# Six edits at once in a float32 transformer block: order of weight sums, blocks of w_out, first loads, 1/rms

## The chip, the cores and the metric

The kernel runs on one core of a Trainium2 chip. The metric is the device time of one execution in microseconds (us); smaller is better. The engines are TensorE (PE; PEld is its weight load), VectorE (DVE), ScalarE (ACT), GpSimd (POOL) and SyncE (SP), whose queue issues most of the transfers (DMA). Each engine runs its instructions in the order in which they stand in its program and waits at an instruction until what it needs is there.

## The reference

One block of a transformer on x of 512 tokens by 1024 features, in float32:

```python
x = x + 0.5 * swiglu(rmsnorm(x, norm_ffn1), w_ffn1_gate, w_ffn1_up, w_ffn1_down)
x = x + hybrid_mixer(rmsnorm(x, norm_mix), w_in, ..., w_out, rel_bias)
x = x + 0.5 * swiglu(rmsnorm(x, norm_ffn2), w_ffn2_gate, w_ffn2_up, w_ffn2_down)
return rmsnorm(x, norm_final)
```

with `swiglu(h) = (silu(h @ w_gate) * (h @ w_up)) @ w_down`, 2816 hidden features (22 blocks of 128). `hybrid_mixer` projects h by `w_in`, runs block-sparse attention (MoBA) on 8 heads and compressed, selected and windowed attention (NSA) on 8 others, heads of 64, and multiplies the concatenated heads by `w_out` (1024 x 1024).

## The kernel before

**Number format.** Each float32 operand is split into two parts, hi (a rounded copy, by ScalarE, line 91 for weights, 226 for the feed-forward pairs) and lo (the rest, by a VectorE subtraction, lines 95 and 227; by GpSimd, line 93, during the mixer). `mm3` (lines 100 to 102) makes one product of three matmuls: hi by hi, hi by lo, lo by hi. A product over 1024 features is 8 `mm3`, 24 matmuls.

**Layout.** x is kept transposed in eight tiles `x0` to `x7` (128 features by 512 tokens). `gained` makes `xo`, the hi and lo of x times the gain of the norm. The factor 1/rms, R, is one number for each token. It is applied after the products, so they can start before R is known: `rms` sums the squares (`acc`) over partitions by four small matmuls `pr` (line 175), takes root and reciprocal, and spreads the result by four transposes `pR` (line 181) and a copy to R (line 182).

**A feed-forward block** (class `Ffn`, twice: `ffn` with wg1, wu1 and with wg2, wu2). Blocks f = 0 to 3 of the hidden features are plain: gate and up products (`pgu`, 24 matmuls of 512 columns each), then times R (`t`, line 281), silu, product with up (line 283), and split into `h` (line 255). The other 18 blocks go in nine pairs by a scheme with seven products for eight (`pair`): VectorE makes sums S1 to S4 of quarters of the weights (`aw`, line 303) and sums of x (`xa`, `xb`, `xc`, `xd`, `th3`, `tl3`), each quarter or sum is split into `sph` and `spl`, and each of 14 steps is 12 matmuls of 256 columns into `pu`, `pv`, `pw`. VectorE puts the results together (lines 327 to 349; line 339 is one such `t`). The down products `pd` of four earlier blocks are mixed between the steps, and line 487 adds each to x. `go` walks over the steps; it issues the loads 12 steps ahead, the sums 6 ahead and the halves 4 ahead. The tiles `aw` rotate through 16 buffers, two pairs' worth.

**The mixer's end.** `w_out(d, k0, k1)` is one of 32 jobs in a list that fills PE's time beside attention: it loads a piece of 128 KB of w_out, splits it (256 columns wide), makes two `mm3` into one bank `pw` and adds it to x (line 774). A job waits until its heads are done. The last eight jobs take heads 4 to 7. `out_halves` splits the result of a head, `po`, into hi and lo of `kvn` by four steps: ScalarE hi (line 819), VectorE difference `to` (820), ScalarE copy `u` of the second part (822), GpSimd sum to lo (823):

```python
            nc.scalar.activation(hi[b], o[:64], AF.Copy)
            nc.vector.tensor_tensor(t[b], o[:64], f32(hi[b]), ALU.subtract)
            nc.scalar.activation(u[b], o[64:], AF.Copy)
            nc.gpsimd.tensor_tensor(lo[b], t[b], u[b], ALU.add)
```

**What sets the order.** A scheduler orders each engine's instructions from the written program; `tc.issue_after(i)` holds what is written under it behind instruction i. At the start SP issues x0, gcol and then in turn quarters of the first gate and up weights and further x; eight matmuls on a tile of ones (`wake`) run on PE before the first product. The raw weights rotate through four buffers, their halves through five.

Of the kernel before, what the change touches and what calls it, by code (L numbers as in the profile page):

```python
# [29 lines left out]
def block_kernel(ctx: ExitStack, tc: tile.TileContext, A: dict, out: bass.AP):  # L30
# [47 lines left out]
    side = [False]  # L78

    def halves(src):  # L80

        n, width = src.shape[1:]
        per = S // width
        out = []
        for k in range(0, n, per):
            m = min(per, n - k)
            hi, lo = [
                wp.tile([128, S], F32R, name=name, tag=name, bufs=bufs)[:, :m * width].rearrange(
                    "p (a b) -> p a b", a=m) for name, bufs in (("whi", 5), ("wlo", 5))]
            v = src[:, k:k + m]  # L90
            nc.scalar.activation(hi, v, AF.Copy)  # L91
# [20 lines left out]
    first_w = [chunk((8, 128)) for _ in range(2)]  # L112
    for k in range(NK):
# [43 lines left out]
    def squares(tmp, k, tag, bufs):  # L157

        if k == 0:
            nc.scalar.activation(acc, xs[k], AF.Square)  # L160
        else:
            s = tmp.tile([128, S], F32, name="sq", tag=tag, bufs=bufs)
            nc.scalar.activation(s, xs[k], AF.Square)
            nc.vector.tensor_tensor(acc, acc, s, ALU.add)

    summed = [None]
    turned_R = [None]

    def rms(ptag):


        with tc.high_priority():
            p = pt(ptag, "pr")
            for i in range(NT):
                summed[0] = nc.tensor.matmul(p[:, i:i + 1], acc[:, i * 128:(i + 1) * 128], ones_f[:, 0:1],
                                             start=True, stop=True)
            nc.scalar.activation(rc, p[:, :NT], AF.Sqrt, bias=eps, scale=1.0 / D)
            nc.vector.reciprocal(rc, rc)
            p = pt(ptag, "pR")
            for i in range(NT):  # L180
                nc.tensor.transpose(p[:, i * 128:(i + 1) * 128], rc[:, i:i + 1].to_broadcast([128, 128]), ident)
            turned_R[0] = nc.scalar.activation(R, p, AF.Copy)
# [4 lines left out]
    class Ffn:  # L187
# [14 lines left out]
        def __init__(self, wg, wu, which, tmp, hp, sp):  # L202
# [3 lines left out]
            self.behind_rms = None  # L206
# [18 lines left out]
        def halves_of_x(self, hi, lo, v):  # L225
            nc.scalar.activation(hi, v, AF.Copy)  # L226
            nc.vector.tensor_tensor(lo, v, f32(hi), ALU.subtract)  # L227
# [30 lines left out]
        def plain(self, f):  # L258
# [10 lines left out]
            def halves_of(m):  # L269
                got[m] = halves(got[m])  # L270
# [18 lines left out]
        def pair(self, f):  # L289
# [8 lines left out]
            def sums(m, name):  # L298
# [4 lines left out]
                nc.vector.tensor_tensor(to, x, y, op)  # L303
# [65 lines left out]
        def down(self, w, fs, then, tag="mm", groups=(1,) * NK):  # L369
# [9 lines left out]
            def halves_of(d):  # L379
                if d % (4 // n) == 0:  # L380
                    i = d * n % 8
                    for k, v in enumerate(halves(raw[d * n // 8][:, i:i + 4])):
                        got[d + k // n, k % n] = v
# [27 lines left out]
        def lay(self, wd):  # L411
# [3 lines left out]
            self.steps += self.down(wd[0], range(FP), half_added, None, (4, 4))  # L415
# [39 lines left out]
    def bias_rows(hp):  # L455
# [14 lines left out]
        def make():  # L470
            nc.vector.tensor_tensor(tabs[0:32, :], tabs[0:32, :], far, ALU.subtract)
            for oh, h0, c, m in parts:
                p = pt(None, "pb")
                nc.tensor.matmul(p[:16 - h0, :m], tabs[:, h0:16], oh[:, :m], start=True, stop=True)
# [14 lines left out]
    with ExitStack() as ph:  # L489
# [6 lines left out]
        for _ in range(8):  # L496
# [5 lines left out]
        ffn.behind_rms = 1, 1  # L502
# [3 lines left out]
        def after(i):  # L506
            if i == 1:
                with tc.issue_after(made[0].ins):
# [42 lines left out]
    with ExitStack() as ph:  # L551
# [81 lines left out]
        def token_major(key, src, width, tiles):  # L633
# [5 lines left out]
            def chunk_of(k0):  # L639
                k1 = min(k0 + per, NK)  # L640

                def body(w):
# [11 lines left out]
                    for i in range(NT):  # L654
# [4 lines left out]
                        if wide < width:  # L659
                            with tc.issue_after(turned_R[0].ins):  # L660
# [105 lines left out]
        def w_out(d, k0, k1):  # L766
            def body(w):
                while any(2 * k + 1 not in out_done for k in range(k0, k1)):
                    yield
                p = pt("mm", "pw")  # L770
                for k in range(k0, k1):
                    mm3(p, w[k - k0], oT[k], k == k0, k == k1 - 1)
                    yield
                nc.vector.tensor_tensor(xs[d], p, xs[d], ALU.add)
                if k1 == 4:
                    got["x", d] = gained(d, 2)
                    squares(tmp, d, "t", 6)
            return A["w_o"][d][:, k0:k1], body
# [27 lines left out]
        def out_halves(h):  # L806
# [16 lines left out]
            nc.gpsimd.tensor_tensor(lo[b], t[b], u[b], ALU.add)  # L823
# [146 lines left out]
        for i in range(4):  # L970
            fill += [proj(2 * i, moba_t("q", i)), proj(2 * i + 1, moba_t("k", i))]
            if i == 2:
                fill += [w_out(d, 4, 6) for d in range(NK)]
        fill += [w_out(d, k, k + 2) for k in (6, 0) for d in range(NK)]
        last = [w_out(d, 2, 4) for d in range(NK)]
# [63 lines left out]
    with ExitStack() as ph:  # L1039
# [5 lines left out]
        ffn.behind_rms = 1, 0  # L1045
# [96 lines left out]
def _laid_out(x, norm_ffn1, w_ffn1_gate, w_ffn1_up, w_ffn1_down, norm_mix, w_in, cmp_pos_k, cmp_w1_k,  # L1142
# [22 lines left out]
        "w_o": _blocks(w_out[0], D, 128),  # L1165
# [29 lines left out]
```

## Time and profile before

| | |
|---|---|
| median of 3 runs | 1009.53 us (1008.88 to 1009.92) |
| profiled execution, its own time | 1011.25 us |
| its span, first to last instruction | 1009.5 us |
| mean granted TensorE clock | 0.996 |
| PE busy | 983.8 us (97%) |
| VectorE busy | 776.9 us (77%) |
| ScalarE busy | 564.9 us (56%) |
| GpSimd busy | 137.3 us (14%) |

The profile is of one execution. Busy is the time in which an engine has an instruction running. Matmuls overlap, and the ends of matmuls are modelled, so a start says more than a duration.

### The profile page before, as it was taken

The page shows a single profiled execution, that of the slowest core. Times are in us where ns is not written, and L with a number is a line of the kernel's source. Part 1 is how long each engine was busy: PE and PEld are TensorE (multiplying, and loading weights), DVE is VectorE, ACT ScalarE, POOL GpSimd, SP SyncE. Part 2 cuts the span into 40 slices and gives each one's busy share as a digit, 9 for nine tenths or more (in the row PEclk, how much of TensorE's full clock was granted, in tenths as well). Part 3 has the DMA queues.
Part 4 walks back from the last instruction along what each step waited for, and adds up shares of the span by engine and source line. Part 5 has one row for each costly group of instructions (what it writes and reads, how often), then busy time and mean ns, then how long its engine had stood idle before and what let it go on. Part 6 is the DMA issues. An engine that isn't in the chain of part 4 may idle for free.

```text
span 1009.5 us, 17013 instructions
## 1 busy us (share of the span) xinstructions
PE 983.8 (97%) x6080; PEld 871.0 (86%) x6080; DVE 776.9 (77%) x1578; ACT 564.9 (56%) x1181; POOL 137.3 (14%) x193
## 2 busy tenths in 40 slices
PE   8999999999999999999999999999999999999996
PEld 6779999999999898787878888788899999999995
DVE  6797888788766488758888978779878888776744
ACT  6463654454444266557677977655455445444436
POOL 0000000000000000036555776300000000000002
PEclk9999999999999999999999999999999999999998
DMA  7254544233501125541011322425244232341102
GB/s 244 87 197 153 186 149 113 98 101 89 161 25 54 45 85 177 165 127 38 20 45 32 93 65 84 140 86 209 69 144 142 86 105 91 120 146 43 33 11 84
DMA packets 53513, 104.53 MB, mean 104 GB/s; under 512 B 10513, under 2 KB 19170, under 8 KB 53428
## 3 DMA queue, kind: packets, MB, share of 16 engines
q1 hardware_dynamic: 53428, 103.44, 32.6%
q8 instruction: 48, 0.79, 0.3%
q14 instruction: 37, 0.30, 0.1%
HBM read 97.98 MB, written 5.30 MB: 102 GB/s over the span
## 4 chain that ended last, share of the span: by engine, by line
PE 82%; DVE 11%; DMA 3%; issue 2%; ACT 1%; POOL 0%; SPq 0%; DVEq 0%; ACTq 0%; POOLq 0%
PE pd L102 6%; PE pd L100 6%; PE pd L101 6%; PE pu L100 6%; PE pu L102 5%; PE pu L101 5%; PE pw L100 4%; PE pw L101 4%; PE pw L102 4%; PE pp L102 3%; PE pgu L100 3%; PE pp L100 3%; PE pp L101 3%; PE pgu L101 3%; PE pv L100 3%; PE pgu L102 3%
## 5 line engine op out<-in xcount | busy, mean ns | idle before, releaser
L226 ACT ACTIVATE sph<-aw 128x512 fp32r<-128x512 f32 x252 | 155.7, 628 | 138.0 <-PE pu L101 68.1
L91 ACT ACTIVATE whi<-raw 128x512 fp32r<-128x512 f32 (+2 forms) x216 | 124.6, 589 | 151.3 <-PE pd L101 71.8
L227 DVE TENSOR_TENSOR spl<-aw,sph 128x512 fp32r<-128x512 f32 x252 | 170.0, 685 | 49.5 <-ACT sph L226 47.9
L101 PE MATMUL pd<-h,whi 128*128 128x512 f32 x336 | 131.9, 392 | 1.4 <-DVE h L255 1.4
L102 PE MATMUL pd<-h,wlo 128*128 128x512 f32 x336 | 130.9, 390 | 0.8 <-DVE wlo L95 0.6
L95 DVE TENSOR_TENSOR wlo<-raw,whi 128x512 fp32r<-128x512 f32 (+1 forms) x168 | 110.9, 671 | 23.9 <-ACT whi L91 22.6
L100 PE MATMUL pd<-h,whi 128*128 128x512 f32 x336 | 129.0, 392 | 0.0
L100 PE MATMUL pu<-th,sph 128*128 128x256 f32 x432 | 121.5, 281 | 1.1 <-DVE t L339 1.1
L303 DVE TENSOR_TENSOR aw<-aw 128x512 f32<-128x512 f32 x144 | 97.6, 683 | 31.7 <-DMA aw<-in_wg 13.6
L102 PE MATMUL pu<-th,spl 128*128 128x256 f32 x432 | 121.1, 280 | 0.0
L101 PE MATMUL pu<-tl,sph 128*128 128x256 f32 x432 | 121.0, 280 | 0.0
L487 DVE SCALAR_TENSOR_TENSOR x<-pd,x 128x512 f32<-128x512 f32 x88 | 59.9, 685 | 44.7 <-PE pd L102 44.4
L100 PEld LDWEIGHTS pu<-th,sph 128*128 128x128 f32 x432 | 81.6, 189 | 2.8 <-DVE t L339 1.3
L101 PEld LDWEIGHTS pu<-tl,sph 128*128 128x128 f32 x432 | 81.9, 190 | 1.1
L100 PE MATMUL pw<-xo,sph 128*128 128x256 f32 x288 | 80.8, 281 | 0.8 <-DVE x L487 0.5
L102 PEld LDWEIGHTS pu<-th,spl 128*128 128x128 f32 x432 | 81.2, 188 | 0.1
L101 PE MATMUL pw<-xo,sph 128*128 128x256 f32 x288 | 80.4, 280 | 0.0
L102 PE MATMUL pw<-xo,spl 128*128 128x256 f32 x288 | 79.7, 280 | 0.0
L102 PEld LDWEIGHTS pd<-h,wlo 128*128 128x128 f32 x336 | 63.1, 188 | 14.1 <-DVE wlo L95 1.2
L101 PEld LDWEIGHTS pd<-h,whi 128*128 128x128 f32 x336 | 63.3, 188 | 12.8 <-DVE h L255 2.2
L100 PEld LDWEIGHTS pd<-h,whi 128*128 128x128 f32 x336 | 62.9, 188 | 11.1
L100 PEld LDWEIGHTS pw<-xo,sph 128*128 128x128 f32 x288 | 54.1, 188 | 2.6 <-ACT sph L226 1.6
(245 smaller groups left out, 2454.5 us busy)
## 6 DMA issues: line engine op xcount, KB each, us to landing
aw<-in_wg SPq DMA_DIRECT2D x72, 256.0 KB, 3.8
aw<-in_wu SPq DMA_DIRECT2D x72, 256.0 KB, 3.6
raw<-in_wd1a SPq DMA_DIRECT2D x20, 512.0 KB, 4.7
raw<-in_wd2a SPq DMA_DIRECT2D x20, 512.0 KB, 4.8
raw<-in_w_a SPq DMA_DIRECT2D x16, 512.0 KB, 4.4
raw<-in_w SPq DMA_DIRECT2D x8, 512.0 KB, 3.7
raw<-in_w_o SPq DMA_DIRECT2D x32, 128.0 KB, 2.2
raw<-in_wg SPq DMA_DIRECT2D x7, 512.0 KB, 3.8
```

Source lines behind the costliest of these rows:

```text
L91: nc.scalar.activation(hi, v, AF.Copy)
L95: nc.vector.tensor_tensor(lo, v, f32(hi), ALU.subtract)
L100: nc.tensor.matmul(p, w[0], v[0], start=first, stop=False, skip_group_check=again)
L101: nc.tensor.matmul(p, w[0], v[1], start=False, stop=False, skip_group_check=again)
L102: nc.tensor.matmul(p, w[1], v[0], start=False, stop=last, skip_group_check=again)
L226: nc.scalar.activation(hi, v, AF.Copy)
L227: nc.vector.tensor_tensor(lo, v, f32(hi), ALU.subtract)
L303: nc.vector.tensor_tensor(to, x, y, op)
L487: nc.vector.scalar_tensor_tensor(xs[d], p, 0.5, xs[d], ALU.mult, ALU.add)
```

## The change

1. The sums of weights (`sums`) and the splitting of the down weights that are mixed among the pairs stand behind the last `lo` written before them (`behind_lo`).
2. w_out is laid out on the host in blocks of 512 KB (four tiles of x by two of k). 32 jobs become 8, `w_out(g, k0, last)`; halves are 512 wide. In the last two jobs the four products of the first k come before those of the second, into banks of two kinds.
3. The lo sum of head 7, the last head, is made by VectorE.
4. ScalarE's queue issues the two halves of the first gate weights; SP issues all of x and then the first up weights. The up weights are split behind the last `xo`, the squares behind that split.
5. 12 wake matmuls for 8.
6. In both feed-forward blocks the `pr` matmuls stand before the fifth `mm3` of f=1's gate product, the `pR` transposes before f=1's up product. (Before: the sums ahead of f=1's up product in the first block, of its gate product in the second, and no place given for the transposes.) The small matmuls `pb` for the bias rows stand behind `pr`.

```diff
@@ first loads
+    for h in four:
+        nc.scalar.dma_start(first_w[0][:, h], A["wg1"][0][:, h])
     for k in range(NK):
...
         if k == 0:
             nc.sync.dma_start(gcol, A["gcol"])
-        if k < 4:
-            i, h = k % 2, slice(4 * (k // 2), 4 * (k // 2) + 4)
-            nc.sync.dma_start(first_w[i][:, h], A[("wg1", "wu1")[i]][0][:, h])
+    for h in four:
+        nc.sync.dma_start(first_w[1][:, h], A["wu1"][0][:, h])
@@ class Ffn
+            self.last_lo = nc.vector.tensor_tensor(lo, v, f32(hi), ALU.subtract)
+        def behind_lo(self):
+            return tc.issue_after(self.last_lo.ins) if self.last_lo else nullcontext()
...
             def run(m):
                 p = got["p", m] = pt(None, "pgu")
-                with tc.issue_after(summed[0].ins) if (f, m) == self.behind_rms else nullcontext():
-                    for k in range(NK):
+                for k in range(NK):
+                    gate = self.rms_at.get((f, m, k))
+                    with tc.issue_after(gate[0].ins) if gate else nullcontext():
                         mm3(p, got[m][k], self.xg[k], k == 0, k == NK - 1)
...
-                nc.vector.tensor_tensor(to, x, y, op)
+                with self.behind_lo():
+                    nc.vector.tensor_tensor(to, x, y, op)
...
-        for _ in range(8):
+        for _ in range(12):
...
-        ffn.behind_rms = 1, 1
+        ffn.x_made = made[0]
+        ffn.rms_at = {(1, 0, 4): summed, (1, 1, 0): turned_R}
...
-            if i == 1:
-                with tc.issue_after(made[0].ins):
+            if i == 0:
+                with tc.issue_after(ffn.first_up.ins):
@@ output projection
-        def w_out(d, k0, k1):
+        def w_out(g, k0, last=False):
             def body(w):
...
+                for i, k in [(i, k) for k in range(2) for i in range(4)] if last else [
+                        (i, k) for i in range(4) for k in range(2)]:
+                    if k == 0:
+                        ps[i] = pt("mm" if not last or i < 2 else "s", "pw")
+                    mm3(ps[i], w[2 * i + k], oT[k0 + k], k == 0, k == 1)
...
-            nc.gpsimd.tensor_tensor(lo[b], t[b], u[b], ALU.add)
+            (nc.vector if h == 7 else nc.gpsimd).tensor_tensor(lo[b], t[b], u[b], ALU.add)
...
-        ffn.behind_rms = 1, 0
+        ffn.rms_at = {(1, 0, 4): summed, (1, 1, 0): turned_R}
```

What the scheduler makes of it on the engines is shown at three places. On PE, ahead of the second plain block of the first feed-forward block, `pr` moved 12 matmuls and `pR` 20 matmuls up.

The first place is VectorE around the split of the last plain block's `h` in the first feed-forward block (`h_641` before, `h_645` after). Before:

```order
L283 TENSOR_TENSOR t_635<-t_635,t_634 128x512
L303 TENSOR_TENSOR aw_870<-aw_870,aw_918 128x512
L217 TENSOR_TENSOR xc_588<-xa_587 128x256
L227 TENSOR_TENSOR xo_675<-xa_587,xo_674 128x256
L303 TENSOR_TENSOR aw_894<-aw_894,aw_942 128x512
L227 TENSOR_TENSOR xo_677<-xb_589,xo_676 128x512
L255 TENSOR_TENSOR h_641<-t_635,h_640 128x512
```

Of the change:

```order
L234 TENSOR_TENSOR spl_761<-aw_444,sph_760 128x512
L234 TENSOR_TENSOR spl_821<-aw_501,sph_820 128x512
L319 TENSOR_TENSOR aw_446<-aw_446,aw_550 128x512
L234 TENSOR_TENSOR spl_826<-aw_548,sph_825 128x512
L319 TENSOR_TENSOR aw_503<-aw_503,aw_607 128x512
L234 TENSOR_TENSOR xo_679<-xc_592,xo_678 128x256
L234 TENSOR_TENSOR spl_831<-aw_605,sph_830 128x512
L266 TENSOR_TENSOR h_645<-t_639,h_644 128x512
```

The sums of the second pair (`aw_870`, `aw_894`) are gone from here; those of the first pair, which stood 9 and 13 rows ahead of `h`, now stand three and five rows ahead, and the four `spl`, which followed `h`, precede it.

The second place is VectorE at the end of the first pair (line 339, after the change line 355, adds a finished product). Before:

```order
L330 TENSOR_TENSOR t_914<-pw_925,wc_998 128x256
L303 TENSOR_TENSOR aw_1161<-aw_1161,aw_1210 128x512
L227 TENSOR_TENSOR spl_1038<-aw_868,sph_1037 128x512
L303 TENSOR_TENSOR aw_868<-aw_870,aw_868 128x512
L303 TENSOR_TENSOR aw_1185<-aw_1185,aw_1234 128x512
L339 TENSOR_TENSOR t_1034<-pu_835,wc_962 128x256
```

Of the change:

```order
L346 TENSOR_TENSOR t_918<-pw_929,wc_1002 128x256
L234 TENSOR_TENSOR spl_1042<-aw_872,sph_1041 128x512
L355 TENSOR_TENSOR t_1038<-pu_839,wc_966 128x256
L234 TENSOR_TENSOR spl_1060<-aw_896,sph_1059 128x512
L319 TENSOR_TENSOR aw_874<-aw_874,aw_922 128x512
L355 TENSOR_TENSOR t_1057<-pu_857,wc_984 128x256
```

The three sums that stood ahead of the finished product's `t` are gone from ahead of it; the sum of the third pair (`aw_1161`) now stands some 35 rows later.

The third place is PE behind the last attention product `po`. Its result becomes `kvn_7521` and `kvn_7522` (hi and lo) before, `kvn_7513` and `kvn_7514` after. Before:

```order
L107 MATMUL po_7529<-tl_7514,vm_4844 128x128
L100 MATMUL pw_7764<-kvn_7421,whi_7718 128x512
L101 MATMUL pw_7764<-kvn_7422,whi_7718 128x512
L102 MATMUL pw_7764<-kvn_7421,wlo_7719 128x512
L100 MATMUL pw_7783<-kvn_7421,whi_7732 128x512
L101 MATMUL pw_7783<-kvn_7422,whi_7732 128x512
L102 MATMUL pw_7783<-kvn_7421,wlo_7733 128x512
L100 MATMUL pw_7764<-kvn_7521,whi_7718 128x512
L100 MATMUL pw_7783<-kvn_7521,whi_7732 128x512
L101 MATMUL pw_7764<-kvn_7522,whi_7718 128x512
```

Of the change, from the seventh matmul behind `po` on (the six ahead of it are of other heads):

```order
L101 MATMUL pw_7680<-kvn_7413,whi_7566 128x512
L102 MATMUL pw_7680<-kvn_7414,whi_7566 128x512
L103 MATMUL pw_7680<-kvn_7413,wlo_7567 128x512
L101 MATMUL pw_7680<-kvn_7513,whi_7566 128x512
L101 MATMUL pw_7688<-kvn_7513,whi_7570 128x512
L101 MATMUL pw_7692<-kvn_7513,whi_7570 128x512
L101 MATMUL pw_7684<-kvn_7413,whi_7566 128x512
L102 MATMUL pw_7684<-kvn_7414,whi_7566 128x512
L103 MATMUL pw_7684<-kvn_7413,wlo_7567 128x512
L101 MATMUL pw_7684<-kvn_7513,whi_7566 128x512
L102 MATMUL pw_7680<-kvn_7514,whi_7566 128x512
```

The first use of lo is the ninth matmul behind `po` before, the seventeenth after. On ScalarE a split of the next feed-forward block's first weights stands between the steps `kvn` and `u` of this head after the change; on VectorE its lo part stands between `to` and the sum.

## Rows read from the trace of the kernel before

**Rows 1.** Page, busy us (share of the span) xinstructions of each engine.

```profile
PE 983.8 (97%) x6080; PEld 871.0 (86%) x6080; DVE 776.9 (77%) x1578; ACT 564.9 (56%) x1181; POOL 137.3 (14%) x193
```

**Rows 2.** Windows: stretch, its length, busy us of each engine, PEclk, DMA share, GB/s.

```profile
50.00:75.00 25.00, 23.52 (x103) 18.76 (x102) 25.00 (x50) 14.79 (x31) 0.00 (x0) 1.00 0.56 203
75.00:100.00 25.00, 23.89 (x177) 22.52 (x176) 19.94 (x36) 8.95 (x18) 0.00 (x0) 1.00 0.44 140
625.00:650.00 25.00, 22.60 (x107) 17.92 (x106) 16.88 (x27) 15.81 (x31) 11.58 (x14) 1.00 0.38 121
700.00:725.00 25.00, 23.81 (x130) 20.05 (x129) 23.13 (x43) 8.05 (x16) 0.00 (x0) 1.00 0.05 15
750.00:775.00 25.00, 23.79 (x185) 22.65 (x185) 19.82 (x37) 13.56 (x30) 0.00 (x0) 1.00 0.44 145
800.00:825.00 25.00, 25.00 (x169) 23.03 (x168) 18.48 (x34) 10.77 (x22) 0.00 (x0) 1.00 0.36 113
```

**Rows 3.** PE's waits: what waited, for what: us in total, times, longest.

```profile
PE pw L101 <- POOL kvn L823: 1.6, 1, 1.6
PE pd L101 <- DVE h L255: 1.4, 2, 1.1
PE pu L100 <- DVE t L339: 1.1, 1, 1.1
PE pv L100 <- ACT sph L226: 0.9, 1, 0.9
```

**Rows 4.** Timeline of VectorE: start, us, instruction [idle before <-releaser].

```profile
66.76 0.67 DVE L303 TENSOR_TENSOR aw<-aw 128x512 f32<-128x512 f32 x1
67.96 0.67 DVE L255 TENSOR_TENSOR h<-t,h 128x512 fp32r<-128x512 f32 x1
```

**Rows 5.** Timeline of PE, the same stretch.

```profile
67.07 1.29 PE L100 MATMUL pd<-h,whi 128*128 128x512 f32 x5
68.69 0.50 PE L101 MATMUL pd<-h,whi 128*128 128x512 f32 x1 [0.32 <-DVE h L255]
```

**Rows 6.** Timeline of VectorE, first use of R.

```profile
32.23 1.29 DVE L281 TENSOR_TENSOR t<-pgu,R 128x512 f32<-128x512 f32 x2 [1.98 <-ACT R L182]
```

**Rows 7.** Timeline of VectorE, end of the first pair.

```profile
96.14 0.69 DVE L303 TENSOR_TENSOR aw<-aw 128x512 f32<-128x512 f32 x1 [1.88 <-DMA aw<-in_wg]
98.68 0.42 DVE L339 TENSOR_TENSOR t<-pu,wc 128x256 f32<-128x256 f32 x1
```

**Rows 8.** Timeline, all engines, behind the last attention product.

```profile
636.31 0.59 ACT L819 ACTIVATE kvn<-po 64x512 fp32r<-64x512 f32 x1 [0.17 <-PE po L107]
637.01 0.68 DVE L820 TENSOR_TENSOR to<-po,kvn 64x512 f32<-64x512 f32 x1 [0.41 <-POOL wlo L93]
637.73 0.59 ACT L822 ACTIVATE u<-po 64x512 f32<-64x512 f32 x1 [0.82 <-DVE to L820]
638.46 1.26 POOL L823 TENSOR_TENSOR kvn<-to,u 64x512 fp32r<-64x512 f32 x1 [1.49 <-ACT u L822]
639.77 0.50 PE L101 MATMUL pw<-kvn,whi 128*128 128x512 f32 x1 [1.60 <-POOL kvn L823]
```

**Rows 9.** Timeline of PE, SP and ScalarE, start of the kernel.

```profile
1.47 3.78 PE L497 MATMUL wake<-ones 128*128 128x512 f32 x8 [1.47 <-DVE ones L136]
...
1.65 0.43 SPq L121 DMA_DIRECT2D raw<-in_wg  x1
...
6.39 0.79 PE L100 MATMUL pgu<-xo,whi 128*128 128x512 f32 x1 [1.15 <-ACT whi L91]
...
12.87 1.38 ACT L147 ACTIVATE xo<-x,gcol 128x512 fp32r<-128x512 f32 x2 [0.19 <-DMA x<-in_xT]
...
19.81 0.39 PE L100 MATMUL pgu<-xo,whi 128*128 128x512 f32 x1
```

**Rows 10.** Chain that ended last, start of the kernel: start, us, what.

```profile
7.61 0.43 PE pgu L102
```

More of the change, by code (lines that the diff above doesn't have):

```diff
@@ L78, in block_kernel @@
     side = [False]
+    last_hi = [None]
     def halves(src):
@@ L163, in squares @@
             nc.scalar.activation(s, xs[k], AF.Square)
-            nc.vector.tensor_tensor(acc, acc, s, ALU.add)
+            added[0] = nc.vector.tensor_tensor(acc, acc, s, ALU.add)
+    added = [None]
     summed = [None]
-    turned_R = [None]
+    turned_R, copied_R = [None], [None]
     def rms(ptag):
@@ L367, in pair, with down @@
             return steps
-        def down(self, w, fs, then, tag="mm", groups=(1,) * NK):
+        def down(self, w, fs, then, tag="mm", groups=(1,) * NK, kept_back=True):
             n = len(fs)
@@ L381, in halves_of @@
                     i = d * n % 8
-                    for k, v in enumerate(halves(raw[d * n // 8][:, i:i + 4])):
+                    with self.behind_lo() if kept_back else nullcontext():
+                        parts = halves(raw[d * n // 8][:, i:i + 4])
+                    for k, v in enumerate(parts):
                         got[d + k // n, k % n] = v
@@ L414, in lay @@
                 self.steps += self.plain(f)
-            self.steps += self.down(wd[0], range(FP), half_added, None, (4, 4))
+            self.steps += self.down(wd[0], range(FP), half_added, None, (4, 4), False)
             fills = []
@@ L470, in make @@
         def make():
-            nc.vector.tensor_tensor(tabs[0:32, :], tabs[0:32, :], far, ALU.subtract)
+            with tc.issue_after(added[0].ins):
+                nc.vector.tensor_tensor(tabs[0:32, :], tabs[0:32, :], far, ALU.subtract)
             for oh, h0, c, m in parts:
                 p = pt(None, "pb")
-                nc.tensor.matmul(p[:16 - h0, :m], tabs[:, h0:16], oh[:, :m], start=True, stop=True)
+                with tc.issue_after(summed[0].ins):
+                    nc.tensor.matmul(p[:16 - h0, :m], tabs[:, h0:16], oh[:, :m], start=True, stop=True)
                 if h0:
@@ L764, in block_kernel @@
         out_done = set()
-        def w_out(d, k0, k1):
+        def w_out(g, k0, last=False):
             def body(w):
-                while any(2 * k + 1 not in out_done for k in range(k0, k1)):
+                while any(2 * k + 1 not in out_done for k in (k0, k0 + 1)):
                     yield
-                p = pt("mm", "pw")
-                for k in range(k0, k1):
-                    mm3(p, w[k - k0], oT[k], k == k0, k == k1 - 1)
-                    yield
[L774 to L778, printed above, removed]
+                ps = {}
+                for i, k in [(i, k) for k in range(2) for i in range(4)] if last else [
[3 more added lines that the diff above has]
+                    mm3(ps[i], w[2 * i + k], oT[k0 + k], k == 0, k == 1)
+                    yield
+                    if k == 1:
+                        d = 4 * g + i
+                        nc.vector.tensor_tensor(xs[d], ps[i], xs[d], ALU.add)
+                        if last:
+                            got["x", d] = gained(d, 2)
+                            squares(tmp, d, "t", 6)
+            return A["w_o"][k0 // 2, g], body
         def stream(jobs, ahead=3):
@@ L972, in block_kernel @@
             if i == 2:
-                fill += [w_out(d, 4, 6) for d in range(NK)]
-        fill += [w_out(d, k, k + 2) for k in (6, 0) for d in range(NK)]
-        last = [w_out(d, 2, 4) for d in range(NK)]
+                fill += [w_out(g, 4) for g in range(2)]
+        fill += [w_out(g, k) for k in (6, 0) for g in range(2)]
+        last = [w_out(g, 2, True) for g in range(2)]
         work = stream(pre + fill + last)
```

22 lines of the change are left out of this document (14 added, 8 removed).

## The prediction

> **What bounds the kernel now.** I read the page first. TensorE (PE) is busy 983.8 of 1009.5 us and VectorE 776.9, ScalarE 564.9 [rows 1], so the time is the sum of the stretches in which PE stands still, and nearly nothing else can be won. The second view is the table of windows. In a steady stretch of the second feed-forward block, 800 to 825, PE is busy the whole 25.00 us; in 50 to 75, 75 to 100, 625 to 650, 700 to 725 and 750 to 775 it lacks 1.48, 1.11, 2.40, 1.19 and 1.21 us [rows 2]. The reader should see in the same rows that VectorE is busy 25.00 of 25 in 50 to 75: there it sets the pace, and PE waits for whatever stands late in VectorE's queue. The third view, the list of PE's waits, gives the names: the lo half of an attention output added on GpSimd (1.6), `h` of the feed-forward blocks (1.4 in two waits), the `t` of line 339 (1.1), `sph` (0.9) [rows 3]. The fourth, the timeline, says why those are late.
>
> **What the change does to each, and its price.** The span is 1009.5 and the run's own time 1011.25, so 1.75 lie outside; this execution is 1.72 above the median of 1009.53. I make the sum against 1011.25 and take 1.72 off at the end.
>
> *The first feed-forward block.* VectorE works in the order of its program. At 66.76 it makes a sum of weights (0.67) for a pair of blocks that is far from due, and only at 67.96 the `h` that the down products need; PE has run five first products ahead from 67.07 and then idles 0.32 [rows 4, 5]. The order's first excerpt shows four such sums within the dozen or so VectorE rows ahead of `h`, at 0.60 each from one start to the next (66.76 to 67.96 is two): 2.4 us, of which two (those of the second pair) now stand some 40 rows later and the other two follow the first `spl` halves. Also, R (1/rms), which starts VectorE's saturated stretch with the first `t` at 32.23 [rows 6], comes earlier: its transposes stand 20 matmuls further up, 20 x 0.225 = 4.5 us. (0.225 is the pitch of 512-column matmuls in a dense stretch: five are shown as 1.29 [rows 5] and one as 0.39 [rows 9], so 0.90 / 4.) VectorE was late by 1 to 3 rows of 0.6; both shifts are larger. So I expect the 1.48 of this window to go.
>
> In the pairs, a sum at 96.14 made VectorE idle 1.88 for the transfer of its operand, though `t` for PE (98.68) stood behind it [rows 7]; PE then waited 1.1 [rows 3]. The second excerpt's `aw_1161` is that sum, ahead of line 339's `t`; it now stands behind the `spl` of the pair's end. What was hidden by it? Nothing: VectorE has 5 us free in that window (19.94 of 25) [rows 2]. So the 1.11 goes too. Together 2.59, taken at nine tenths: **-2.3** (bounds -1.0, if only the waits behind a transfer go, and -2.6).
>
> *The second block* has the same two places: 1.19 and 1.21 [rows 2]. R gains nothing relative to PE here, since its transposes already stood ahead of the up products; only the sums move. **-2.2** of 2.40 (bounds -0.6 and -2.4).
>
> *The end of the output projection.* After the last attention product the chain is ScalarE 636.31, VectorE 637.01, ScalarE 637.73, GpSimd 638.46 to 639.72, and PE takes it at 639.77: 3.5 us, which eight matmuls (1.8) were meant to cover, and PE waits 1.60 [rows 8]. Now the add is on VectorE. For a 64x512 add there I take 0.68, the duration of VectorE's own 64x512 step in the same chain, against GpSimd's 1.26 [rows 8]: -0.58 on the path. And by the third excerpt sixteen matmuls stand in the gap instead of eight: 3.6 us. Against this, two instructions that the diff doesn't show have slid in: ScalarE's `whi` of the next block's first weights stands between the chain's two ScalarE steps, waiting for PE's last use of a buffer, five matmuls (1.1) behind the last `po`, and then about 0.6, like ScalarE's other 512-wide steps there; VectorE's `wlo` of it (0.6) stands ahead of the add. The chain is then about 1.2 + 0.6 + 0.6 + 0.1 + 0.68 = 3.2, or about 3.3 with `u` beside it, against 3.6: covered, by 0.3. If the cover fails, the 512-wide blocks give nothing here. Of the 2.40 of this window I take **-1.9** (bounds 0 and -2.4); the rest are waits for `x` of line 774, whose 0.68 adds remain.
>
> *The blocks of w_out* themselves: 32 transfers become 8, the same bytes; ScalarE and GpSimd make half as many halves of twice the width. GpSimd's 512-wide step I price at the 1.26 of the 64x512 one. It lies beside PE; cost 0 unless it holds up a scaled softmax row behind it, at most 1.26 a time.
>
> *The start.* Real products begin at 6.39; the first matmul of block f=1 at 19.81; 48 matmuls lie between them, 10.8 us at 0.225, so 2.6 us are lost to waiting and to the slow pitch of 0.43 that the chain shows at first [rows 10], about twice 0.225, as at the lower of TensorE's two levels (1.2 GHz). The gate's weights were issued third, at 1.65, and the last x was awaited at 12.87 [rows 9]. Now ScalarE's queue issues the gate's weights at the very start and up's 512 KB go behind all x. Gate's 24 products then follow x as it lands, and up's 24 (5.4) start when its weights have landed and been halved. The bytes are the same, so the last still land about 12.9 less the two issues of 0.43 saved; 12.0 to 12.9 plus about 0.6 for one half plus 5.4 is 18.0 to 18.9, and a little more, as the last matmuls of the gate may still run. Twelve wake matmuls instead of eight add 4 x 0.43 = 1.7 to the 3.78 us of waking [rows 9, 10] and close the idle 1.15 ahead of the first product; they cost nothing while ScalarE's first `whi` and `xo` are what PE awaits. The two new issues on ScalarE lie in time that it spent waiting for gcol. f=1 at 18.9: **-0.9** (bounds 0, PE stopping once between gate and up, and -1.6).
> The Trainium skill speaks against part of this: "DMA: Bandwidth & Descriptors" (Issuing engines are not separate DMA queues) says that transfers from several issuing engines share the same 16 DMA engines and that only issue time is saved. By that rule alone, with up's weights landing no sooner than the last x did, the start gains about 0.4 and the time would be 1001.8. No row of before has two issuing engines, so the trace doesn't decide it.
>
> *Earlier summed squares.* The four `pr` stand twelve matmuls (2.7 us) further up, and with f=1 0.9 earlier they could meet an unfinished sum of squares: cost 0 to 0.5, inside the start's bounds.
>
> *Restarts.* Each wait costs PE more than the idle shown: five matmuls from 67.07 at 0.225 would let the next start at 68.20; it starts at 68.69, 0.49 later, where 0.32 is shown [rows 5]. Some eight waits go, at about 0.15, three quarters of it: **-0.9** (0 to -1.2).
>
> Sum: -0.9 -2.3 -2.2 -1.9 -0.9 = -8.2. 1011.25 - 8.2 = 1003.05 for an execution like the profiled one; less 1.72: **1001.3**. All upper bounds together: -10.2, 999.3. All lower: -1.6, 1007.9.
>
> **Rivals.** *Half of it* (0.15): VectorE's lateness in the two dense stretches only moves. For it: VectorE is full in 50 to 75, and no edit removes work from it. Against: R comes earlier, and two sums leave the stretch. The feed-forward terms halve, -2.3, and half of the restarts go: about 1004.
> *The projection's cover fails* (0.12): the slid-in `whi` waits longer than five matmuls, for its weights' transfer, and holds `u` behind it. For it: in before the same weights were issued only at about the time of the last `po`; against: a buffer of the 8 large jobs comes free a whole job (24 matmuls, 5.4 us) earlier. Then the 1.9 stays: 1003.2.
> *The start gains nothing* (0.13): the bytes bound it: 1002.2.
> *Slower* (0.07): a sum held behind the last `spl` comes too late for ScalarE's `sph`, and as ScalarE too works in order, every half behind it is late. There are 18 pairs in the two blocks; it decides once a pair loses 0.46 us (8.2 / 18). With 0.7 a pair, 12.6 in all, the time is 1001.3 + 12.6 = 1013.9. Against: sums are asked for six steps ahead and halves four, two steps of 12 matmuls of 256 columns, at half of 0.225, 2.7 us, and VectorE has 20% to spare outside the dense stretch.
> *No effect* (0.03): the sums' place in the queue is not what makes PE wait: 1009.5 within 0.2%, which is 2 us and about what a measurement of this kernel can tell from no change.
>
> **How the numbers follow.** The forecast, 999 to 1003, has 0.50; the three partial rivals 0.40 end between 1002 and 1004.5, or with two of them together near 1006. The range 998.3 to 1006.5 goes from the full bounds, with 1 us for the spread of the runs shown, to two partial failures at once. Faster by over 0.2% (below 1007.5): 0.88; within: 0.05 (no effect, and what is left when the partial ones come together); slower: 0.07.
>
> **What would show it.** Windows 50 to 75 and 75 to 100 (and their like in the second block) with PE near 25.0; no wait of `pd` for `h`, of `pu` for line 339's successor, of `pw` for the lo add. No VectorE idle on an `aw` transfer with `t` behind it. First matmul of f=1 at about 18.9. I'm wrong if a new entry over 1 us heads PE's waits, above all `sph` or `aw` at every pair, or ScalarE's `whi` after the last `po`.

## The result, and the profile after

| | median us | runs | ratio to the kernel before, 95% interval |
|---|---|---|---|
| before | 1009.35 | 1008.88 to 1009.92 (4) | |
| changed | 998.98 | 997.14 to 999.69 (4) | 0.990 (0.9888 to 0.9911) |

The change takes 10.4 us off, 1.0%. The forecast was 1001.3 (8.2 less), range 998.3 to 1006.5. The measured median lies just below the stretch of 999 to 1003 that had the chance of 0.50, and below 999.3, all upper bounds of the sum together; the range holds it because it adds 1 us for the spread of the runs. The profiled execution took 999.69 us, its span is 997.9.

The page's line of busy times (us, share of the span, instructions; [rows 1]):

```profile
PE 979.2 (98%) x6084; PEld 870.7 (87%) x6084; DVE 780.9 (78%) x1579; ACT 566.3 (57%) x1165; POOL 132.6 (13%) x176
```

PE is busy 4.6 us less than before in a span that is 11.6 shorter. The table of windows, with the stretches of [rows 2]:

```profile
50.00:75.00 25.00, 25.00 (x121) 21.03 (x120) 25.00 (x48) 15.01 (x31) 0.00 (x0) 1.00 0.48 171
75.00:100.00 25.00, 25.00 (x195) 24.15 (x194) 17.29 (x31) 11.85 (x24) 0.00 (x0) 1.00 0.54 175
625.00:650.00 25.00, 25.00 (x115) 20.57 (x114) 20.74 (x35) 16.52 (x29) 2.58 (x2) 1.00 0.20 64
700.00:725.00 25.00, 25.00 (x182) 23.58 (x181) 19.34 (x34) 9.81 (x20) 0.00 (x0) 1.00 0.36 108
750.00:775.00 25.00, 24.00 (x176) 22.65 (x177) 23.49 (x43) 15.12 (x30) 0.00 (x0) 1.00 0.41 127
800.00:825.00 25.00, 25.00 (x177) 23.36 (x176) 20.36 (x36) 13.07 (x26) 0.00 (x0) 1.00 0.20 64
```

Four of the five stretches that lacked 1.1 to 2.4 us of PE are full. One wait of about an us is left in 750 to 775. PE's longest waits, to be held against [rows 3]:

```profile
PE wake L517 <- DVE ones L139: 1.5, 1, 1.5
PE ps_t L916 <- DVE th L977: 1.3, 2, 1.0
PE ps_t L916 <- DVE tl L920: 1.2, 1, 1.2
PE pu L101 <- ACT t L361: 1.1, 1, 1.1
PE ps_s L892 <- DVE m L898: 1.1, 6, 0.2
```

None of the four of [rows 3] is there. `ps_t` for `tl`, 1.2, is new and lies in attention; `pu` for ScalarE's `t`, 1.1, is new too, at 751.00. VectorE no longer stands idle ahead of the sums of weights. The page's lines, before and changed (us busy, mean ns of one, then us of idle before them and what ended most of it):

```profile
L303 DVE TENSOR_TENSOR aw<-aw 128x512 f32<-128x512 f32 x144 | 97.6, 683 | 31.7 <-DMA aw<-in_wg 13.6
L319 DVE TENSOR_TENSOR aw<-aw 128x512 f32<-128x512 f32 x144 | 98.2, 683 | 0.0
```

At the start (ScalarE's and SP's queues and PE; [rows 9]):

```profile
0.74 0.90 ACTq L116 DMA_DIRECT2D raw<-in_wg  x2
...
1.47 4.53 PE L517 MATMUL wake<-ones 128*128 128x512 f32 x12 [1.47 <-DVE ones L139]
...
6.11 0.99 SPq L124 DMA_DIRECT2D raw<-in_wu  x2
...
18.41 0.39 PE L101 MATMUL pgu<-xo,whi 128*128 128x512 f32 x1
```

Block f=1 begins at 18.41, 1.40 earlier.

A better view than idle times is where the same matmul of PE stands in time. The table gives, from the timeline of PE, five stretches between such landmarks: **S**, from 0 to the first `pgu` matmul of f=1; **A**, from the first `pd` to the first `pp` (the rest of the first feed-forward block); **M**, from there to the last `po` (mixer); **P**, from there to the 25th `pgu` matmul of the second block (end of the output projection); **F**, from that block's first `pd` to the last.

| | S | A | M | P | F |
|---|---|---|---|---|---|
| before | 19.81 | 303.37 | 275.76 | 19.82 | 305.63 |
| changed | 18.41 | 297.75 | 276.47 | 16.69 | 302.99 |
| difference | -1.40 | -5.62 | +0.71 | -3.13 | -2.64 |
| the prediction's terms | -0.9 | -2.3 | 0 | -1.9 | -2.2 |

The prediction's remaining -0.9 was for restarts in A, P and F.

### The profile page after: what moved, and what is told of

Same layout as the page of the kernel before. It is cut to its first block, busy times and chain, and to the rows that moved or that the text cites. A ratio compares the mean times of both kernels' runs of the same rounds, so it can differ in the third digit from the quotient of the medians.

```text
span 997.9 us, 16910 instructions
## 1 busy us (share of the span) xinstructions
PE 979.2 (98%) x6084; PEld 870.7 (87%) x6084; DVE 780.9 (78%) x1579; ACT 566.3 (57%) x1165; POOL 132.6 (13%) x176
## 4 chain that ended last, share of the span: by engine, by line
PE 92%; DVE 4%; ACT 1%; DMA 1%; issue 1%; SPq 0%; ACTq 0%; DVEq 0%
PE pd L101 8%; PE pd L102 8%; PE pd L103 8%; PE pu L101 6%; PE pu L103 6%; PE pu L102 6%; PE pw L101 5%; PE pw L102 4%; PE pw L103 4%; PE pp L103 3%; PE pgu L101 3%; PE pgu L102 3%; PE pp L101 3%; PE pgu L103 3%; PE pp L102 3%; PE pv L101 3%
## 5 line engine op out<-in xcount | busy, mean ns | idle before, releaser
L233 ACT ACTIVATE sph<-aw 128x512 fp32r<-128x512 f32 x252 | 157.7, 630 | 158.6 <-PE pu L102 74.6
L92 ACT ACTIVATE whi<-raw 128x512 fp32r<-128x512 f32 (+1 forms) x200 | 122.1, 621 | 174.7 <-PE pd L102 88.4
```

The lines of the kernel that those rows point to most:

```text
L92: last_hi[0] = nc.scalar.activation(hi, v, AF.Copy)
```

## The experiments

All medians stand beside those of the kernel before on the same chip, 1009.58 for e1 to e4, 1009.96 for e5 to e8, 1009.78 for e9 to e12. Two versions whose intervals overlap are not told apart by their medians; for these the landmarks of one profile each are given, as what they are. Of the landmarks P and A repeat well where the same code runs: P is 16.69 to 16.71 in seven profiles and 19.81 to 19.86 in four, A 297.63 to 298.09 in the nine that have edits 1 and 6. S and M vary more (see e9 and the last section).

**e1: the order of the sums undone.**

```diff
-                with self.behind_lo():
-                    nc.vector.tensor_tensor(to, x, y, op)
+                nc.vector.tensor_tensor(to, x, y, op)
...
-                    with self.behind_lo() if kept_back else nullcontext():
-                        parts = halves(raw[d * n // 8][:, i:i + 4])
+                    parts = halves(raw[d * n // 8][:, i:i + 4])
```

> The changed kernel with the sums and the kept-back down halves again wherever the scheduler puts them (edit 1 undone), all else kept. Theory A, the place of the sums in VectorE's queue is what made PE wait: of the 8.2 us that the two feed-forward blocks gained (landmarks of PE: 5.6 in the first, 2.6 in the second), 5 to 8 come back, about 1004 to 1007, and waits of PE for h and for t behind a transfer of aw are in the list again. Theory B, the earlier R relieved VectorE and the sums' place is a side matter: 0 to 3 come back, 999 to 1002, and the pairs behind the first stay dense.

1004.23 us, ratio 0.9944 (0.9923 to 0.9964). A is 301.76 (+4.0 against the changed kernel), F 304.73 (+1.7). From PE's waits:

```profile
PE pd L102 <- DVE h L266: 1.8, 2, 0.9
...
PE pu L101 <- DVE t L363: 0.8, 2, 0.6
...
PE pv L103 <- DVE spl L234: 0.7, 2, 0.4
```

Theory A, at its lower edge. The 4.0 are spread: 1.6 us in the dense stretch up to the first pair's middle, 2.4 in the pairs behind it, in waits for `t` and `spl` that end at 120.74, 123.21 and 152.66 and smaller ones.

**e2: edit 6 undone, the rest kept.**

```diff
-        ffn.rms_at = {(1, 0, 4): summed, (1, 1, 0): turned_R}
+        ffn.rms_at = {(1, 1, 0): summed}      # first block
+        ffn.rms_at = {(1, 0, 0): summed}      # second block
```

(the places of the bias products go back as well)

> The changed kernel with edit 6 undone: sums of squares again ahead of the first block's up product of f=1 and of the second block's gate product, no place for the transposes. Theory A: VectorE's dense stretch of the first block (50 to 87) starts later against PE and about 1 to 2 us come back, all of it ahead of the first pair's second half; the second block is unchanged; 1000 to 1001. Theory B: 2.5 us or more come back, 1001.5 or above. If the sums alone suffice: under 0.5 us.

1005.94 us, ratio 0.9964 (0.9952 to 0.9976): 7.0 above the changed kernel's median, 6.5 by the two ratios. Only theory B's open bound (2.5 us or more) holds, and it named no place; theory A held the second block unchanged. A is 301.12, +3.4, of which 2.3 at `h` and 0.7 at a `wlo` behind it. The other half is in a place that I had not thought of, the second block:

```profile
PE pr L179 <- DVE acc L167: 2.0, 1, 2.0
PE pd L102 <- DVE h L266: 2.0, 1, 2.0
```

The windows around it (columns as in [rows 2]; PEclk is the third number from the end):

```profile
657.00:660.00 3.00, 2.09 (x13) 1.86 (x14) 1.04 (x3) 1.01 (x2) 0.00 (x0) 0.95 0.58 175
660.00:663.00 3.00, 3.00 (x9) 2.35 (x8) 0.00 (x0) 0.00 (x0) 0.00 (x0) 0.50 0.03 5
663.00:675.00 12.00, 12.00 (x56) 9.95 (x55) 9.12 (x16) 6.96 (x11) 0.00 (x0) 0.99 0.26 76
```

With the projection's end 3.1 shorter, PE comes to `pr` before the sum of squares is made: it waits 2.0 us, and then its granted clock is 0.50 for about 3.4 us: 9 matmuls in 3 us, where 13 or 14 fit. P is as short as after the change (16.70), but the stretch behind it up to the first `pd` takes 43.3 instead of 39.5. So in this block the edit does not move R ahead, as the first block's does; it moves `pr` twelve matmuls **back**, out of the way of a wait that the faster projection would have made.

**e5 and e6: each of the two alone, on the kernel before.**

> The kernel before with edit 1 alone. With e1 and e2 read: behind the first dense stretch the sums' place alone should bring what e1 lost there, 2.5 to 3 us in the first block's pairs and 1 to 2 in the second block; in the dense stretch of 56 to 77 nothing or a loss, as in e2, where PE waited 2.1 for h. Theory A (place and earlier R help different stretches and only together free the dense one): 1005.5 to 1007.5. Theory B (the place of the sums suffices): 1003 or below.

> The kernel before with edit 6 alone. Theory A: the dense stretch of the first block gains 1 to 2 us, the pairs nothing; in the second block the dense stretch (707 to 714) keeps its wait for h, since R stood ahead of it before too: 1007.5 to 1009. Theory B: the earlier R also moves the pairs' waits: 1005 or below.

e5: 1003.47, ratio 0.9938 (0.9922 to 0.9953), A 299.72 (-3.7 against before), F 301.76 (-3.9). e6: 1008.82, ratio 0.9989 (0.9977 to 1.0002), A 302.96 (-0.4), F 305.14 (-0.5). Their waits, e5 first:

```profile
PE pw L102 <- POOL kvn L841: 1.6, 1, 1.6
...
PE pd L102 <- DVE h L265: 1.0, 1, 1.0
```

```profile
PE pu L101 <- DVE t L353: 2.9, 3, 1.3
...
PE pd L102 <- DVE h L265: 1.6, 2, 0.9
```

The order alone already gives 6.5 us, near theory B's 1003 and below the range of theory A, because the pairs gained more than the 2.5 to 3 expected. The first block shows it in two parts. From the first `pd` to the 197th matmul behind it (in the middle of the first pair, where each kernel has made the same products) the order alone gains 0.3 us on before, the earlier R alone 0.9, both (changed kernel) 2.2. From there to the first `pp` it is 3.3, -0.5 and 3.4. So the gain in the pairs is the order's, and in the dense stretch theory A holds: with the order alone PE still waits 1.0 for `h` there; with the earlier R alone it waits 0.6 (the rest of the 1.6 is in the second block), and 2.9 for `t` in the pairs of both blocks. Only with both (changed kernel, e10) is there no wait for `h`. VectorE's idle time ahead of the sums is 31.6 us in e1 and 27.4 in e6, and 0.0 in e5 as in every other run with the order. e6's gain is not shown by its median.

**e10: the two together, nothing else** (before, with edits 1 and 6).

> The kernel before with edits 1 and 6 together and nothing else. Alone they gave 6.5 and 1.1 in the medians, 7.6. Theory A, they free different stretches and the dense one only together: 7.5 to 9 below before, 1001 to 1002.5. Theory B, with the old start R's gain is not used, since PE too is late: 6.5 or less, 1003.5 or above.

999.88 us, ratio 0.9910 (0.9893 to 0.9927). Above both expectations in its gain: 9.9 us, of 10.4 for all six; e5 and e6 sum to 7.6. By the medians alone this excess is not clear of the intervals; in A the two give 3.7 and 0.4 alone and 5.7 together, in F 3.9 and 0.5 alone and 3.6 together, so it lies in the first block's dense stretch. A is 297.63, the changed kernel's value. P is 19.86, as before. So two edits carry the change; that the other four add something is not shown by the medians (their intervals overlap), though the profile has P 3.2 longer here. Its M is 3.0 shorter than the changed kernel's: 1.6 for a dip of the clock (last section), 1.4 that the blocks cost in attention (e8).

**e3, e4, e9: the start.** e3 undoes edit 4 (the diff's load lines, and the squares behind `made[0]` again), e4 edit 5 (`range(8)`), e9 both.

> The changed kernel with edit 4 undone: gate and up weights again issued by SP between the x, products in turns, squares as before; 12 wake matmuls are kept. My theory: the order of the bytes ahead of x and up gave most of the 1.4 us by which block f=1 starts earlier: 0.8 to 1.4 come back, 999.8 to 1000.4. Rival: the longer waking gave it, by an earlier rise of the pitch, and this run loses under 0.5.

> The changed kernel with 8 wake matmuls. My theory: PE idles about 0.9 between waking and the first product, its pitch stays at 0.43 until about 10 us, but the loads bound the start, so block f=1 starts 0 to 0.6 later: 999.0 to 999.6. Rival: the lower pitch now bounds the gate's products, f=1 starts 1 us or more later: 1000 or above.

> The changed kernel with edits 4 and 5 both undone (8 wake matmuls, weights and x in turns on SP). Undone one by one they cost 0.64 and 0.99 at the start of block f=1 and nothing measurable in the median. Theory A: each alone keeps PE at the short pitch from about 5 us on, both away leave it at 0.43 until 10 us or later, as in before, e5 and e6; f=1 then starts 1.4 to 3 us later (19.8 to 21.5), R comes later too, and 1.5 to 3 us come back: 1000.5 to 1002. Theory B: they simply add, 1.6 at f=1, under 1 us in the median.

Medians 999.13 (ratio 0.9901, 0.9879 to 0.9922), 998.49 (0.9889, 0.9866 to 0.9912) and 999.25 (0.9905, 0.9887 to 0.9924): none can be told from the changed kernel, so the 0.8 to 1.4 expected of e3 did not come. In the profiles f=1 begins at 19.40, 19.05 and 21.52, against 18.41. e9's windows, then the changed kernel's:

```profile
4.00:8.00 4.00, 2.39 (x8) 1.07 (x7) 2.20 (x3) 1.82 (x3) 0.00 (x0) 0.97 0.85 296
8.00:12.00 4.00, 4.00 (x8) 2.48 (x9) 2.93 (x5) 3.68 (x7) 0.00 (x0) 0.50 1.02 381
12.00:16.00 4.00, 4.00 (x13) 3.16 (x13) 3.81 (x7) 3.96 (x8) 0.00 (x0) 0.68 0.91 316
```

```profile
4.00:8.00 4.00, 3.46 (x11) 1.92 (x10) 2.55 (x4) 3.21 (x6) 0.00 (x0) 1.00 1.05 359
8.00:12.00 4.00, 3.86 (x17) 3.08 (x18) 4.00 (x7) 3.63 (x6) 0.00 (x0) 1.00 1.01 340
12.00:16.00 4.00, 4.00 (x19) 3.15 (x18) 2.95 (x6) 3.70 (x8) 0.00 (x0) 1.00 0.79 261
```

With both undone PE's granted clock is 0.50 in 8 to 12, and 8 matmuls start in it instead of 17. e3 and e4 have 12 and 14 there, at a granted clock of 1.00. In the five profiles with the old start (before, e5, e6, e9, e10) f=1 begins at 19.81, 21.21, 21.50, 21.52 and 19.63; in the six with both edits and edit 6 (changed, e1, e7, e8, e11, e12) between 18.41 and 19.00. Either edit is enough for the clock (theory A's mechanism, in one profile each), yet its price in the median, 1.5 to 3, did not come. In e9's profile the later start is not lost on the way: its first `pd` is 2.9 us later than the changed kernel's, its first `pp` 3.2, its last `pd` 2.3. But this is the slowest of e9's six executions (1002.25, mean granted clock 0.990; the others 997.35 to 1001.14 at 0.995 to 0.997), so the profile overstates what the old start costs, and f=1 begins anywhere from 19.63 to 21.52 with it. What it costs in the median is open.

**e7, e11: the end of the projection.** e7 undoes edit 2 (32 jobs of 128 KB), e11 edit 3:

```diff
-            (nc.vector if h == 7 else nc.gpsimd).tensor_tensor(lo[b], t[b], u[b], ALU.add)
+            nc.gpsimd.tensor_tensor(lo[b], t[b], u[b], ALU.add)
```

> The changed kernel with w_out in 32 jobs of 128 KB again (edit 2 undone); head 7's lo sum stays on VectorE. My theory: the wait behind the last attention product comes back less the 0.6 that VectorE's add saves (1.0 to 1.2 of the 1.6), with a wait or two for x: of the 3.1 us won between the last po and the second block's products 1.5 to 2.5 come back; ahead of it, in attention, 0.5 to 1 is won back, as GpSimd's 512-wide steps no longer hold VectorE. 1000 to 1001. Rival, the blocks themselves do nothing for the time and the add did it all: 998 to 999.

> The changed kernel with head 7's lo sum on GpSimd (edit 3 undone). Between the last po and PE's first use of lo stand sixteen matmuls, 3.6 us; the chain of the changed kernel measured against them has to be lengthened by 0.58. If the prediction's chain of 3.2 to 3.3 is right, PE waits 0.2 to 0.4 and the projection's end comes 0.2 to 0.5 later. Rival: the blocks cover it all, no wait. In the median 999 to 999.5, or not to be told from the changed kernel.

e7: 998.23 (ratio 0.9892, 0.9875 to 0.9909), e11: 998.21 (0.9890, 0.9874 to 0.9907); neither median can be told from the changed kernel. P is 19.24 and 17.13, against 16.69 with both edits and 19.82 with neither. So the add alone takes 0.58, the difference between 1.26 and 0.68 of the prediction; the blocks alone 2.69; both 3.13. In the median e7's 1000 to 1001 did not come, and the rival's 998 to 999 did, but not for its reason: the blocks do win at the end. Their waits:

```profile
PE pw L102 <- DVE kvn L845: 1.0, 1, 1.0
...
PE pw L101 <- DVE x L795: 0.8, 2, 0.5
```

```profile
PE pw L102 <- POOL kvn L851: 0.3, 1, 0.3
```

The chain in the changed kernel (all engines, [rows 8]):

```profile
630.15 0.59 ACT L846 ACTIVATE kvn<-po 64x512 fp32r<-64x512 f32 x1 [1.67 <-PE po L108]
...
630.84 0.69 DVE L847 TENSOR_TENSOR to<-po,kvn 64x512 f32<-64x512 f32 x1 [0.41 <-ACT kvn L846]
...
631.40 0.64 ACT L92 ACTIVATE whi<-raw 128x512 fp32r<-128x512 f32 x1 [0.66 <-PE pw L102]
...
632.06 0.59 ACT L849 ACTIVATE u<-po 64x512 f32<-64x512 f32 x1
...
632.19 0.68 DVE L96 TENSOR_TENSOR wlo<-raw,whi 128x512 fp32r<-128x512 f32 x1
...
632.91 0.69 DVE L851 TENSOR_TENSOR kvn<-to,u 64x512 fp32r<-64x512 f32 x1
...
633.43 0.39 PE L101 MATMUL pw<-kvn,whi 128*128 128x512 f32 x1
...
633.74 0.47 PE L102 MATMUL pw<-kvn,whi 128*128 128x512 f32 x1
```

The `whi` and `wlo` that slid in are there, at 631.40 and 632.19, each ahead of a step of the chain. PE's first use of lo starts 0.31 behind the matmul ahead of it, 0.08 more than the pitch: the cover of 3.6 us is used up to the last tenth, where I counted on 0.3 to spare.

And yet e7 is not slower. Its M is 275.14 against 276.47. The blocks give back in attention a part of what they win at the end, and e8 says how. Without the clock's dip (last section) M is 274.89 with the blocks (e4) and 273.49 to 273.65 with small jobs (e5, e6, e10): the blocks cost 1.2 to 1.4 there.

**e8: GpSimd's lo in two halves.**

```diff
-                nc.gpsimd.tensor_tensor(lo, v, f32(hi), ALU.subtract)
+                for c in range(0, m, 2):
+                    nc.gpsimd.tensor_tensor(lo[:, c:c + 2], v[:, c:c + 2], f32(hi[:, c:c + 2]), ALU.subtract)
```

> The changed kernel; GpSimd makes each lo of 512 columns by two instructions of 256. My theory: a VectorE instruction with two operands in SBUF that meets one of GpSimd's waits for its end (aq of line 609 took 1.70 instead of 0.69 beside a GpSimd lo of 1.29); with halves of 0.74 it waits less, 1.2 or below, and PE's wait of 1.2 for tl behind it falls to 0.7 or below; 998.0 to 998.8. Rival, the lengthening has another cause: aq stays at 1.7 and the wait at 1.2.

997.42 us, ratio 0.9879 (0.9862 to 0.9895). The changed kernel's timeline where `ps_t` waits for `tl`, then e8's at the same place:

```profile
594.34 1.29 POOL L94 TENSOR_TENSOR wlo<-raw,whi 128x512 fp32r<-128x512 f32 x1
...
594.48 1.70 DVE L609 TENSOR_TENSOR aq<-t,aq 64x512 fp32r<-64x512 f32 x1
...
596.94 0.69 DVE L609 TENSOR_TENSOR aq<-t,aq 64x512 fp32r<-64x512 f32 x1
...
598.37 0.41 PE L916 MATMUL ps_t<-ident,lpn 128*128 128x128 f32 x2 [1.17 <-DVE tl L920]
```

```profile
592.24 1.88 POOL L95 TENSOR_TENSOR wlo<-raw,whi 128x256 fp32r<-128x256 f32 x2
...
592.38 1.14 DVE L610 TENSOR_TENSOR aq<-t,aq 64x512 fp32r<-64x512 f32 x1
...
595.71 0.41 PE L917 MATMUL ps_t<-ident,lpn 128*128 128x128 f32 x2 [0.60 <-DVE tl L921]
```

In the changed kernel `aq` runs 1.70 beside GpSimd's 1.29 and ends 0.55 behind its end; the next `aq`, 2.5 us later, with no such instruction beside it, takes 0.69. In e8 it takes 1.14, its neighbour being a step of half the width, and PE's wait for `tl` falls from 1.17 to 0.60. The theory's numbers for `aq` and the wait came; the median is below its 998.0 to 998.8, and cannot be told from the changed kernel's. M is 273.81, 1.1 less than in e4, which has no dip of the clock either. That the cause is operands of both engines in SBUF (the memory in which the kernel's tiles lie; products lie in PSUM) fits the other meetings in the changed kernel's trace (last section), but was not tried by itself.

**e12: a version made from the runs.** 128 KB jobs for all but the last eight pieces (`w_small`, the old body on the new layout), blocks for the last two jobs, and e8's halves.

> A version made from the runs: the changed kernel with 128 KB jobs for the first 24 pieces of w_out, as before, and the 512 KB blocks only for the last two jobs; GpSimd's lo of 512 columns in two halves. Theory: attention keeps what e7 and e8 showed (0.6 to 1.3 us), the projection's end keeps its 3.1: 996.8 to 998.0, below both kernels. Rival: the small jobs bring back the wait of 1.1 for t at the end of attention that before and e7 have, and the gain is nil: 998.5 to 999.5.

997.03 us, ratio 0.9878 (0.9862 to 0.9895), the lowest median. It beats the kernel before; its interval touches that of the changed kernel (0.9888 to 0.9911), and e8 is as good. P is 16.18, M 274.62, so it kept P's gain (though PE waits 0.8 for head 7's lo again, at 632.03), but in M, where it was to keep 0.6 to 1.3, it is only 0.3 below e4's 274.89 and behind e8's 273.81; why is open.

## Why the prediction was right, and where its steps were off

*What bounds the kernel.* Right: the gain is PE's waits, which went where the windows had them. Most of it is the order of the sums.

*First feed-forward block, -2.3 and a share of -0.9 for restarts: measured -5.62.* It lies beyond the term's bound of -2.6, even with all of the restarts. The mechanism in the pairs was right, the size was off: I took 1.11 for them, and e5 shows 3.3 by the order alone, from the first pair's middle to the last. I priced it by PE's idle time in two windows. The windows 100 to 125 and 125 to 150 of before show PE busy 24.94 and 25.00 of 25, and yet the same matmuls that take 35.83 us there (102.59 to 138.42) take 34.47 after the change. Eight starts in there come 0.1 to 0.2 late, 1.0 in all, and show as nearly no idle time, since the modelled ends of the matmuls cover them.

In the dense stretch the step "VectorE was late by 1 to 3 rows; both shifts are larger" failed as an argument: the two shifts are not alternatives (0.3 and 0.9 alone, 2.2 together). e5 shows the order alone leaving 1.0 of waiting for `h`, e6 and e1 the earlier R alone leaving 0.6 and 0.9 for it. R comes 4.9 us earlier, but the last `h` only 2.0 (67.96 before, 65.92 after): it follows VectorE's first `t` by 35.7 before and 38.5 after, and by 39.8 in e1 and e6, without the order. With the late R, VectorE's first `t` and that 197th matmul of PE lie 60.6 us apart before (32.23 to 92.81), 59.7 in e2 (33.10 to 92.83) and 60.3 in e5, whenever PE begins; only with edits 1 and 6 together does PE become the bound again: in all nine profiles that have both it takes 33.7 from its first `pd` to that matmul. So a start that is earlier for PE alone is worth nothing there: e2 begins the down products 0.7 earlier than before does and is at 92.83 in the place where before is at 92.81.

*Second block, -2.2: measured -2.64,* and 3.3 to 4.0 in ten other profiles with the sums ordered (F 301.60 to 302.30): the profile of the changed kernel has a wait of 1.1 at 751.00, behind ScalarE's `whi` that waits 3.93 for a transfer of down weights; in e3, e5 and e11 it is not in the list, in e8 and e12 it is 0.4. "The same two places" was a misreading for 750 to 775: of before's 1.21 there, 0.87 is a wait for ScalarE's `sph`, which stands behind a `whi` that waited 1.57 for down weights, and 0.34 one for `spl`. The wait that is left is of the same kind, in ScalarE's queue, although edit 1 also holds that `whi` back behind a `lo`. "R gains nothing relative to PE here" was true for the kernel before, and missed what e2 shows: with the faster projection the old place of `pr` would have cost 3.8 us. This interaction of edits 2 and 6 was in no rival.

*End of the projection, -1.9: measured -3.13.* Right in the mechanism: 0.58 for the add (e7), the rest for the blocks. I took four fifths of the window's 2.40, since I expected waits for `x` to stay; they went too, and the gain is beyond even the bound of -2.4, so here too the idle time was less than the loss. The chain took 3.45 (630.15 to 633.60) for my 3.2 or 3.3. The rival "cover fails" was closer than its 0.12: the margin is nothing.

*The blocks themselves, "cost 0 unless ...".* This term was mis-sized, and by another mechanism than the one named. Not a softmax row behind GpSimd's longer step in its own queue, but VectorE beside it: with the same dip of the clock (below), M is 276.47 against 275.76 and 275.14 with small jobs, 0.7 to 1.3 us; without it 1.2 to 1.4, of which e8 gives 1.1 back.

*Start, -0.9: measured -1.40* in the one pair of profiles, but the medians of e3, e4 and e9 don't show it. That the Trainium skill's "DMA: Bandwidth & Descriptors" (Issuing engines are not separate DMA queues) leaves only issue time to gain is neither borne out nor refuted here: e3, with the old queues and twelve wake matmuls, starts f=1 0.99 later, and no run had the new order of bytes on one queue.

*The rivals.* "Slower", a loss at each of 18 pairs, found nothing: `sph` and `aw` are not in the list of waits. "Half of it" did not come: both feed-forward terms came out larger than taken. "The start gains nothing" is not decided: the medians cannot tell. "No effect" is excluded by the interval.

*The sum.* The blocks' cost and the three terms that came out beyond their bounds do not cancel in the profile (11.6 us for 8.2); that 998.98 still lies in the range is due to the 1 us added for the spread, not to the terms.

## What to carry to other kernels

In an engine that works in order, look for instructions that wait for a transfer and are due much later, and put them behind the last thing somebody waits for; here this alone was 6.5 of 10.4 us. Look at each engine's queue: the wait left at 751.00 is the same thing on ScalarE. Price a wait by where the same instruction of the bound engine stands before and after, not by its idle time: small waits don't show as idle. And when a stretch becomes faster, ask which instruction placed "safely early" behind it now comes too early, as `pr` did.

## What the runs showed of the hardware that was not expected

*The granted clock of PE within a run.* In the profiles of before, changed, e1, e2, e3, e7, e9 and e11 the granted clock falls to half for 3.4 us near 410 us, in e4, e5, e6, e8, e10 and e12 not. Two windows of the kernel before (the second is at 0.51):

```profile
407.00:413.50 6.50, 5.07 (x27) 3.96 (x26) 6.43 (x15) 2.93 (x9) 0.00 (x0) 1.00 0.06 15
413.50:417.00 3.50, 3.50 (x15) 3.11 (x14) 2.61 (x6) 1.26 (x2) 0.00 (x0) 0.51 0.83 241
```

In 407 to 413.5, ahead of it, PE stood still for 1.4 of 6.5 us. That alone does not decide it: in the 6.5 us at the same distance from the first `pp` all fourteen profiles have the same 27 matmuls and 1.42 to 1.44 us of standing still, and eight of them the dip. Counted from the first `pp`, the first `ps_t` behind it starts at 86.72 to 86.79 in the eight and at 85.19 to 85.22 in the six: the dip costs 1.5 to 1.6 us, as much as most of the edits. (e3 and e9 have a second one of 3.4 us at 467 and 469.) So one profile each cannot compare two spans to better than that. The 45 executions of the kernel before beside the experiments fit this: the 20 with a mean granted clock of 0.997 or more have a median of 1008.4 us, the 25 with 0.996 or less 1010.6.

*VectorE beside GpSimd.* A VectorE instruction that takes 0.69 us alone took 1.70 beside a GpSimd one of 1.29, and 1.14 beside half of it. In the changed kernel's trace ten steps of `aq` and `ak`, which read and write SBUF alone, run beside a GpSimd tensor_tensor for over 0.3 us: they take 0.69 to 1.70, 1.17 in the middle, against 0.67 to 0.69 with nothing beside them. Fifteen steps of `x<-pw` and `tl<-ps_t`, which read one operand from PSUM, keep 0.66 to 0.69 beside one.
